# Modulation vectors by VectorE accumulation instead of TensorE products, in a two-layer diffusion trunk step

## The chip, the core and the metric

The kernel runs on one core of a Trainium2 chip, as one program. The metric is the device time of one execution in microseconds (us), as the median of three runs. Five engines work side by side: TensorE (PE in the profile; its weight loads are PEld), VectorE (DVE), ScalarE (ACT), GpSimd (POOL) and SyncE (SP), which here issues every DMA.

## The reference

Two segments of tokens, 128 context tokens and 512 latent tokens, pass the same two layers. Each segment has a conditioning vector; `adaln` turns it into six modulation vectors of 1024 per layer, which scale and shift what goes into the token mixer and the channel mixer and gate what comes out.

```
def adaln(cond, w, b):
    m = jax.nn.silu(cond) @ w + b                       # (1, 1024) @ (1024, 6 * 1024)
    return [m[:, None, i * D_MODEL:(i + 1) * D_MODEL] for i in range(N_MOD)]

def channel_mixer(hn, l, P):
    u = dwconv3(hn @ P['w_up'][l], P['conv_w'][l], P['conv_b'][l])
    val, gate = u[..., :D_FF], u[..., D_FF:]
    return (jax.nn.silu(gate) * val) @ P['w_down'][l]

def trunk_layer(x, mods, l, P, angs, ctx_k, ctx_v):
    sh1, sc1, g1, sh2, sc2, g2 = mods
    hn = rmsnorm(x, P['norm1_g'][l]) * (1 + sc1) + sh1
    mix, k, v = token_mixer(hn, l, P, angs, ctx_k, ctx_v)   # Fourier mixer + differential attention, gated
    x = x + g1 * mix
    hn = rmsnorm(x, P['norm2_g'][l]) * (1 + sc2) + sh2
    x = x + g2 * channel_mixer(hn, l, P)
    return x, k, v
```

## The kernel before

Activations lie transposed, channels on partitions and all 640 tokens along the free axis, in 53 general buffers ("slots", 128 x 640 in float32) that are handed out and taken back in turn. Every large product is computed in three float32r terms (high x high, high x low, low x high). A weight block of 1 MB is loaded into one of two raw tiles (`w_raw`), then split into `w_h` (ScalarE or GpSimd, line 311 or 313) and `w_l` (VectorE, line 317), four pieces of 128 x 512 each. `make_plan` lists the blocks in order; a block is loaded when the block two places ahead of it has been used (`pump_loads`).

The program goes, for each layer, through: a prologue or `layer_start` (norm, first key/query/value products), eight attention heads, the gate products with the Fourier mixer woven in, `merge`, `w_o`, then up and down products of the channel mixer in three rounds. TensorE's products are emitted in generators and loops that call `tick()` after each group of matmuls (one k-step of `proj`: six matmuls of 128 x 320); a tick emits one piece of the next weight's split and one of the waiting epilogue operations. In a head, softmax units of four steps alternate with stretches of the next projections as filler; how much filler stands between two steps is set by `cost(h)`. The order written there is a priority: the tile scheduler that builds the program places instructions in each engine's queue by it and by its own estimate of when each can start.

The modulation vectors of layer 0's first norm come from the prologue (`first_ada`). The other 20 blocks of 512 columns (8 of layer 0, 12 of layer 1) are cut in halves of 512 rows. A half is a 1 MB block in the same plan and the same two raw tiles as the weights. It is used unsplit: four matmuls in full float32, with 32 columns of `c_cond` as the stationary operand, each written to its own 32 partitions of a PSUM tile.

```
for j in range(4):
    self.mm(out=ps[32 * j:32 * j + 32, 0:512], lhsT=self.cs[:, 4 * r + j, :], rhs=w[j], tile_position=(0, 32 * j))
```

ScalarE copies the first half's sums out (line 407), VectorE adds the second's (line 411), and `columns` transposes the result back to channels on partitions (four transposes, lines 270 and 429). One half follows each key/query job, value job, Fourier-input job and gate job while there are any (`ada_next`), and in layer 0 also each weight block of the up jobs 1 to 4. So in each layer 12 halves (six blocks) stand in the heads and 4 in the gates, and 8 more in layer 0's up jobs.

The tables of rotary angles and of the Fourier matrices (`c_big`, 1280 KB) are loaded once and stay.

## Time and profile before

| | |
|---|---|
| median of three runs | 2242.63 us (2241.78 to 2243.69) |
| the profiled execution | 2242.44 us, of which 2240.7 us from its first to its last instruction |
| TensorE busy | 2185.7 us, 98% of the span |
| VectorE, ScalarE, GpSimd busy | 1225.3, 800.2 and 362.4 us |
| moved by DMA | 200.41 MB |

The 1.7 us outside the span are there in every execution, so a change of the span is a change of the time. Matmuls are pipelined: one that is shown with 0.31 us starts about 0.147 us after the one before it. What a group of matmuls costs is therefore read from start to start, and the busy time of a group in the listings is time in which at least one of them ran.

### The profile page before, as it was taken

The page shows a single profiled execution, that of the slowest core. Times are in us where ns is not written, and L with a number is a line of the kernel's source. Part 1 is how long each engine was busy: PE and PEld are TensorE (multiplying, and loading weights), DVE is VectorE, ACT ScalarE, POOL GpSimd, SP SyncE. Part 2 cuts the span into 40 slices and gives each one's busy share as a digit, 9 for nine tenths or more (in the row PEclk, how much of TensorE's full clock was granted, in tenths as well). Part 3 has the DMA queues.
Part 4 walks back from the last instruction along what each step waited for, and adds up shares of the span by engine and source line. Part 5 has one row for each costly group of instructions (what it writes and reads, how often), then busy time and mean ns, then how long its engine had stood idle before and what let it go on. Part 6 is the DMA issues. An engine that isn't in the chain of part 4 may idle for free.

```text
span 2240.7 us, 36749 instructions
## 1 busy us (share of the span) xinstructions
PE 2185.7 (98%) x15142; PEld 2102.7 (94%) x15142; DVE 1225.3 (55%) x2258; ACT 800.2 (36%) x1601; POOL 362.4 (16%) x560
## 2 busy tenths in 40 slices
PE   7999999999999999999999999999999999999998
PEld 5988989999999999999989888899999999999997
DVE  5776675225456544545476766742344765355454
ACT  4565564212134221313246666532211433122221
POOL 2122122001032000000051211210010410000001
PEclk9999999999999999999999999999999999999999
DMA  8222322222213332122212222222222122222221
GB/s 312 84 84 84 118 79 76 113 94 71 73 66 113 133 112 76 62 90 76 76 66 102 83 82 85 79 112 99 91 76 76 59 76 75 75 77 75 76 76 47
DMA packets 40631, 200.41 MB, mean 89 GB/s; under 512 B 4496, under 2 KB 12048, under 8 KB 19344
## 3 DMA queue, kind: packets, MB, share of 16 engines
q1 hardware_dynamic: 40464, 198.07, 25.1%
q8 instruction: 119, 1.95, 0.4%
q14 instruction: 48, 0.39, 0.1%
HBM read 193.33 MB, written 4.72 MB: 88 GB/s over the span
## 4 chain that ended last, share of the span: by engine, by line
PE 76%; issue 7%; DVE 5%; POOL 5%; ACT 5%; DMA 1%; SPq 0%; POOLq 0%; ACTq 0%; DVEq 0%
PE ps_d L267 43%; PE ps_t L267 16%; PE ps_s L267 16%; POOL slot L500 2%; POOL ors L703 1%; ACT slot L634 1%; PE ps_t L270 1%; DVE nm L632 1%; DMA slot<-in_w_first 1%; ACT slot L536 1%; ACT junk L701 1%; DVE slot L515 1%; POOL oms L702 1%; ACT slot L537 1%; DVE w_l L317 1%
## 5 line engine op out<-in xcount | busy, mean ns | idle before, releaser
L267 PE MATMUL ps_d<-slot,w_h 128*128 128x320 f32 x5056 | 983.5, 313 | 8.0 <-DVE slot L501 4.5
L267 PEld LDWEIGHTS ps_d<-slot,w_h 128*128 128x128 f32 x5056 | 795.5, 188 | 25.0 <-DVE slot L501 8.4
L267 PE MATMUL ps_d<-slot,w_l 128*128 128x320 f32 x2528 | 595.6, 310 | 2.6 <-DVE w_l L317 2.6
L317 DVE TENSOR_TENSOR w_l<-w_raw,w_h 128x512 fp32r<-128x512 f32 x520 | 360.9, 704 | 264.5 <-ACT w_h L311 155.1
L267 PEld LDWEIGHTS ps_d<-slot,w_l 128*128 128x128 f32 x2528 | 427.8, 188 | 2.9 <-DVE w_l L317 2.9
L311 ACT CAST w_h<-w_raw 128x512 fp32r<-128x512 f32 x308 | 188.3, 620 | 460.2 <-PE ps_d L267 236.0
L313 POOL TENSOR_SCALAR w_h<-w_raw 128x512 fp32r<-128x512 f32 x212 | 143.8, 680 | 1216.5 <-PE ps_d L267 626.9
L267 PE MATMUL ps_s<-slot,w_h 128*128 128x320 f32 x1376 | 265.2, 310 | 0.0
L267 PE MATMUL ps_t<-slot,w_h 128*128 128x320 f32 x1376 | 264.6, 309 | 0.0
L267 PEld LDWEIGHTS ps_t<-slot,w_h 128*128 128x128 f32 x1376 | 217.7, 188 | 1.7 <-ACT slot L945 0.8
L267 PEld LDWEIGHTS ps_s<-slot,w_h 128*128 128x128 f32 x1376 | 217.5, 188 | 1.7 <-ACT slot L945 1.7
L634 ACT ACTIVATE slot<-ps_s,nm 128x640 f32<-128x640 f32 (+1 forms) x160 | 113.7, 711 | 150.2 <-DVE nm L632 148.3
L267 PE MATMUL ps_s<-slot,w_l 128*128 128x320 f32 x688 | 164.9, 310 | 1.1 <-DVE w_l L317 1.1
L267 PE MATMUL ps_t<-slot,w_l 128*128 128x320 f32 x688 | 164.7, 309 | 0.0
L632 DVE TENSOR_REDUCE nm<-ps_s 128x1 f32<-128x640 f32 (+1 forms) x160 | 113.9, 712 | 56.7 <-PE ps_s L267 49.6
L267 PEld LDWEIGHTS ps_s<-slot,w_l 128*128 128x128 f32 x688 | 116.9, 188 | 1.6 <-DVE w_l L317 1.6
L940 DVE SCALAR_TENSOR_TENSOR slot<-ps_d,c_vecs,slot 128x511 f32<-128x511 f32 (+1 forms) x176 | 84.6, 541 | 60.7 <-ACT slot L945 60.7
L267 PEld LDWEIGHTS ps_t<-slot,w_l 128*128 128x128 f32 x688 | 117.0, 188 | 0.0
L267 PE MATMUL ps_s<-slot,slot 128*128 128x320 f32 x512 | 102.3, 322 | 10.2 <-ACT slot L634 10.1
L267 PEld LDWEIGHTS ps_s<-slot,slot 128*128 128x128 f32 x512 | 77.7, 189 | 30.6 <-ACT slot L634 19.3
L267 PE MATMUL ps_d<-w_h,slot 128*128 128x256 f32 x480 | 99.6, 288 | 0.6 <-DVE cols L429 0.6
L940 DVE SCALAR_TENSOR_TENSOR slot<-ps_s,c_vecs,slot 128x511 f32<-128x511 f32 x88 | 42.6, 542 | 87.3 <-ACT slot L945 87.3
(167 smaller groups left out, 2258.9 us busy)
## 6 DMA issues: line engine op xcount, KB each, us to landing
w_raw<-in_w_stream SPq DMA_DIRECT2D x164, 1024.0 KB, 4.9
slot<-in_w_first SPq DMA_DIRECT2D x32, 256.0 KB, 6.0
w_raw<-in_w_stream SPq DMA_DIRECT2D x8, 768.0 KB, 4.3
slot<-in_x_t SPq DMA_DIRECT2D x8, 320.0 KB, 6.2
out_y_t<-slot SPq DMA_DIRECT2D x8, 320.0 KB, 2.2
c_big<-in_t_big SPq DMA_DIRECT2D x1, 1280.0 KB, 9.4
slot<-in_k_t SPq DMA_DIRECT2D x16, 64.0 KB, 1.8
slot<-in_v_h SPq DMA_DIRECT2D x16, 64.0 KB, 1.9
```

The costliest lines, as they stand in the source:

```text
L267: return self.nc.tensor.matmul(**a)
L270: return self.nc.tensor.transpose(*a)
L311: nc.scalar.copy(out=h[:, a:b], in_=raw[:, a:b])
L313: nc.gpsimd.tensor_scalar(out=h[:, a:b], in0=raw[:, a:b], scalar1=1.0, scalar2=0.0, op0=ALU.mult, op1=ALU.add)
L317: nc.vector.tensor_sub(out=lo[:, a:b], in0=raw[:, a:b], in1=h[:, a:b].bitcast(F32))
L500: (eng or nc.gpsimd).tensor_scalar(out=tmp[:, a:b], in0=tmp[:, a:b], scalar1=A, scalar2=B, op0=ALU.mult, op1=ALU.add)
L515: lambda: nc.vector.stream_shuffle(tmp[:, 128:640], src, mask=SHUF),
L536: nc.scalar.copy(out=KD[m][a:b], in_=kr[a:b])
L537: nc.scalar.copy(out=KD[m][c:d], in_=kr[a:b])
L632: nc.vector.tensor_reduce(out=st["nm"][:, m:m + 1], in_=s_ap, axis=AX.X, op=ALU.max, negate=True)
L634: nc.scalar.activation(out=p[:, 0:n], in_=s_ap, func=AF.Exp, bias=st["nm"][:, m:m + 1], scale=1.0, accum_out=st["sum"][:, m:m + 1])
L940: nc.vector.scalar_tensor_tensor(out=y[:, o0:o1], in0=ps[:, 192 + i0:192 + i1], scalar=w, in1=y[:, o0:o1], op0=ALU.mult, op1=ALU.add)
```

## The change

The 40 halves leave the plan and TensorE. The weights of the modulation vectors become an input of their own (`w_ada`, 160 pieces of 128 x 512, 256 KB each), which passes a ring of four slots. For each piece and each of the two segments one step is emitted (`ada_step`): the piece times the segment's conditioning column, added to an accumulator of 128 x 512. The first of a block's eight pieces goes to ScalarE (a scaled copy), the other seven to VectorE (`scalar_tensor_tensor`). That makes 280 steps on VectorE and 40 on ScalarE. After two blocks, TensorE sums the four accumulators over partitions with four matmuls against 32 columns of ones, ScalarE copies the sums out, and four transposes bring both blocks back (`ada_rows`, `ada_columns`): ten times in all.

Steps are emitted in two kinds of stretch alone. In the gates of each layer 0.85 of one comes with each tick, for six blocks. In layer 0's channel mixer 0.25 of one comes with each tick, for eight blocks, and `ada_until` emits what is left before the last down round. The heads have no such work any more, and `cost(h)` loses its 1.2. The tables move to five slots, are given back after use and loaded again at the end of layer 0; there are 61 slots instead of 53.

```diff
-NSLOT = 53
+NSLOT = 61
...
+ADA_UPTO = ((6, 14), (20, 20))
+ADA_RATE = (.85, .25)
...
-    def ada(l, cb):
-        return [(("ada", l, cb, r), "ada", "w_ada", l, 512 * r, 4, [(512 * cb, 512)]) for r in range(2)]
...
+ADA = [(0, cb) for cb in range(4, 12)] + [(1, cb) for cb in (2, 3, 0, 1)] + [(1, cb) for cb in range(4, 12)]
...
+    def tables(self):
+
+        b = self.big = [self.alloc() for _ in range(5)]
+        for i, t in enumerate(b):
+            self.nc.sync.dma_start(out=t[:, 0:512], in_=self.I["t_big"][:, 512 * i:512 * i + 512])
...
         if self.q:
             self.q.popleft()()
+        self.beat += 1
+        self.ada_tick()
...
+    def ada_open(self, upto, rate):
+
+        self.ada_upto, self.ada_rate = 8 * upto, rate
+        if self.ada_n < self.ada_upto:
+            self.ada_ring = [self.alloc() for _ in range(4)]
+            self.ada_at = self.ada_n
+            for _ in range(4):
+                self.ada_load()
+
+    def ada_load(self):
+        n = self.ada_at
+        if n < self.ada_upto:
+            self.nc.sync.dma_start(out=self.ada_ring[n % 4][:, 0:512], in_=self.I["w_ada"][n // 8, n % 8])
+            self.ada_at += 1
+
+    def ada_step(self):
...
+        acc, x = self.ada_acc[2 * (b % 2) + c][:, 0:512], self.cs[:, k, c:c + 1]
+        if k == 0:
+            nc.scalar.activation(out=acc, in_=w, func=AF.Copy, scale=x)
+        else:
+            nc.vector.scalar_tensor_tensor(out=acc, in0=w, scalar=x, in1=acc, op0=ALU.mult, op1=ALU.add)
+        self.ada_c = 1 - c
+        if c:
+            self.ada_n += 1
+            self.ada_load()
+            if k == 7 and b % 2:
+                self.ada_sums.append((self.beat + 10, lambda b=b, acc=self.ada_acc: self.ada_rows(b - 1, acc)))
...
+    def ada_rows(self, b, acc):
+        nc = self.nc
+        ps, s = self.psq(), self.alloc()
         for j in range(4):
-            self.mm(out=ps[32 * j:32 * j + 32, 0:512], lhsT=self.cs[:, 4 * r + j, :], rhs=w[j], tile_position=(0, 32 * j))
...
+            self.mm(out=ps[32 * j:32 * j + 32, 0:512], lhsT=self.one, rhs=acc[j][:, 0:512], tile_position=(0, 32 * j))
+        self.give(*acc)
+        nc.scalar.copy(out=s[:, 0:512], in_=ps[:, 0:512])
+        self.ada_sums.append((self.beat + 3, lambda: self.ada_columns(b, ps, s)))
...
+    def ada_tick(self):
+        if self.ada_sums and self.beat >= self.ada_sums[0][0]:
+            self.ada_sums.popleft()[1]()
+        self.ada_credit += 0 if self.hold else self.ada_rate
+        if self.ada_credit >= 1:
+            self.ada_credit -= 1
+            self.ada_step()
...
-        yield from self.ada_next()
...
-        cost = lambda h: 1.2 + (13.1 + (7.9 if h % 2 == 0 else 5.3) if h < 6 else 13.1 if h == 6 else 26.2)
+        cost = lambda h: (13.1 + (7.9 if h % 2 == 0 else 5.3) if h < 6 else 13.1 if h == 6 else 26.2)
...
+        self.ada_open(ADA_UPTO[l][0], ADA_RATE[0])
         G = gates()
...
+        self.ada_until(ADA_UPTO[l][0])
         self.finish_a(l, 1)
...
+        self.ada_open(ADA_UPTO[l][1], ADA_RATE[1])
         self.ff = [None] * NFF
         self.up_first(l, hn2, hooks)
         for j in range(1, 5):
             self.up(l, j, hn2)
+        self.ada_until(8)
         self.down(l, 0)
...
         if l + 1 < DEPTH:
+            self.ada_until(ADA_UPTO[l][1])
+            self.tables()
```

The first place is TensorE's queue in the gates of layer 0, at the end of a gate job (`w_l` and `w_h` are its weights, `c_big` a Fourier table). Before:

```order
L267 MATMUL ps_d<-slot_519,w_h_93 128x320
L267 MATMUL ps_d<-slot_518,w_l_95 128x320 x2
L267 MATMUL ps_s<-w_raw_92,c_cond 32x512 x4
L267 MATMUL ps_t<-c_big,slot_4683 128x256 x4
L267 MATMUL ps_t<-c_big,xp 128x128 x2
L267 MATMUL ps_d<-slot_264,w_h_94 128x320
```

The same queue in the change, at the end of the third gate job, where the sums of the first two blocks stand (`c_one` are the ones, the slots the accumulators):

```order
L263 MATMUL ps_d<-slot_526,w_l_94 128x320 x2
L263 MATMUL ps_d<-slot_4098,c_one 32x512
L263 MATMUL ps_d<-slot_4099,c_one 32x512
L263 MATMUL ps_d<-slot_4311,c_one 32x512
L263 MATMUL ps_d<-slot_4312,c_one 32x512
L263 MATMUL ps_d<-slot_263,w_h_93 128x320
```

A half after each gate job is replaced by one such group for two whole blocks; there are three groups in the gates of a layer.

The second place is VectorE's queue in the last head, where softmax steps (maximum, reciprocal, factor, combination) take turns with splits. Before:

```order
L632 TENSOR_REDUCE nm<-ps_s 128x1
L643 RECIPROCAL r<-sum 128x2
L644 TENSOR_SCALAR c<-sum,r,c_lam_85 128x1
L646 SCALAR_TENSOR_TENSOR slot_3824<-slot_3825,c,slot_3824 128x640
L704 TENSOR_SCALAR on<-ps_t,r,ors 128x128
L317 TENSOR_TENSOR w_l_95<-w_raw_91,w_h_93 128x512
```

In the change, the last unit of the same head:

```order
L415 SCALAR_TENSOR_TENSOR slot_4099<-slot_4076,c_cond,slot_4099 128x512
L667 TENSOR_REDUCE nm<-ps_s 128x1
L415 SCALAR_TENSOR_TENSOR slot_4099<-slot_4077,c_cond,slot_4099 128x512
L313 TENSOR_TENSOR w_l_95<-w_raw_91,w_h_93 128x512
L678 RECIPROCAL r<-sum 128x2
L415 SCALAR_TENSOR_TENSOR slot_4099<-slot_4078,c_cond,slot_4099 128x512
L679 TENSOR_SCALAR c<-sum,r,c_lam_84 128x1
L415 SCALAR_TENSOR_TENSOR slot_4098<-slot_4075,c_cond,slot_4098 128x512
L681 SCALAR_TENSOR_TENSOR slot_3986<-slot_3987,c,slot_3986 128x640
L739 TENSOR_SCALAR on<-ps_t,r,ors 128x128
```

The scheduler has drawn the first steps of the gates forward, in between the links of the last softmax chain (seven of them up to this place).

The third place is SyncE's queue in the gates of layer 0. Before, it holds the alternating raw tiles alone, weights and halves in turn:

```order
L291 DMA w_raw_91<-in_w_stream 128x2048
L531 DMA out_state_kt<-kp 128x128
L291 DMA w_raw_92<-in_w_stream 128x2048
L291 DMA w_raw_91<-in_w_stream 128x2048 x2
L291 DMA w_raw_92<-in_w_stream 128x2048 x2
```

In the change:

```order
L399 DMA slot_4075<-in_w_ada 128x512
L399 DMA slot_4076<-in_w_ada 128x512
L399 DMA slot_4077<-in_w_ada 128x512
L399 DMA slot_4078<-in_w_ada 128x512
L287 DMA w_raw_91<-in_w_stream 128x2048
L399 DMA slot_4075<-in_w_ada 128x512
```

Eight to twelve loads of the ring, each of which waits for the steps that read the piece before, now stand between two loads of a weight block.

## Rows read from the trace of the kernel before

**Rows 1.** The page: the span, and each engine's busy time.
```profile
span 2240.7 us, 36749 instructions
PE 2185.7 (98%) x15142; PEld 2102.7 (94%) x15142; DVE 1225.3 (55%) x2258; ACT 800.2 (36%) x1601; POOL 362.4 (16%) x560
```

**Rows 2.** TensorE's waits over the whole span: waiting line, releaser, total, times, longest.
```profile
PE ps_s L267 <- ACT slot L634: 10.1, 17, 1.8
PE ps_t L270 <- DVE on L704: 7.4, 12, 0.8
...
PE ps_d L270 <- DVE slot L411: 2.9, 6, 0.6
```

**Rows 3.** TensorE's groups by line and shape: the halves, each of eight records.
```profile
L267 PE MATMUL ps_d<-w_raw,c_cond 128*32 128x512 f32 x256 | 36.2, 605 | 0.0
...
L267 PE MATMUL ps_s<-w_raw,c_cond 128*32 128x512 f32 x32 | 4.3, 605 | 0.0
L267 PE MATMUL ps_t<-w_raw,c_cond 128*32 128x512 f32 x32 | 4.3, 604 | 0.0
```

**Rows 4.** TensorE's timeline around one half in the gates (start, duration).
```profile
397.08 0.45 PE L267 MATMUL ps_d<-slot,w_l 128*128 128x320 f32 x2
...
398.50 0.86 PE L267 MATMUL ps_d<-slot,w_h 128*128 128x320 f32 x4
```

**Rows 5.** TensorE's timeline at one block's four transposes in the gates.
```profile
420.90 0.60 PE L270 MATMUL ps_d<-c_small,slot 128*128 128x128 f32 x4
421.26 0.83 PE L267 MATMUL ps_d<-slot,w_h 128*128 128x320 f32 x4
```

**Rows 6.** Windows of heads 2, 5, 6, layer 0: length; busy PE, PEld, DVE, ACT, POOL; clock; DMA.
```profile
146.94:183.56 36.62, 35.99 (x273) 34.25 (x272) 26.93 (x52) 22.27 (x55) 7.64 (x12) 1.00 0.33 114
...
261.06:301.40 40.34, 37.74 (x284) 34.65 (x282) 26.18 (x52) 24.57 (x63) 7.85 (x14) 1.00 0.19 66
301.40:333.57 32.17, 30.62 (x206) 26.79 (x206) 24.67 (x49) 20.20 (x54) 6.77 (x11) 1.00 0.29 98
```

**Rows 7.** VectorE's groups by line and shape (busy, mean ns; idle before, releasers).
```profile
L317 DVE TENSOR_TENSOR w_l<-w_raw,w_h 128x512 fp32r<-128x512 f32 x520 | 360.9, 704 | 264.5 <-ACT w_h L311 155.1 <-POOL w_h L313 107.3 <-PE ps_d L267 1.5
...
L646 DVE SCALAR_TENSOR_TENSOR slot<-slot,c,slot 128x640 f32<-128x640 f32 x64 | 57.9, 905 | 1.9
...
L567 DVE SCALAR_TENSOR_TENSOR slot<-slot,slot 64x512 fp32r<-64x512 f32 x32 | 21.9, 686 | 3.9 <-ACT slot L562 3.1
```

**Rows 8.** Windows of layer 0's gates and of its first up jobs, columns as in rows 6.
```profile
384.00:512.00 128.00, 128.00 (x870) 122.79 (x870) 32.06 (x64) 32.98 (x55) 9.41 (x15) 1.00 0.25 91
690.00:830.00 140.00, 140.00 (x960) 131.72 (x959) 80.34 (x147) 43.03 (x60) 12.76 (x18) 1.00 0.36 131
```

**Rows 9.** The chain that ended last: one Fourier group's products, one gate job.
```profile
404.05 1.44 PE ps_s L267 x12
...
409.12 2.17 PE ps_t L267 x12
...
440.91 14.08 PE ps_d L267 x96
```

**Rows 10.** Timelines of GpSimd and of VectorE in the seventh head.
```profile
326.95 1.28 POOL L517 TENSOR_TENSOR slot<-slot,c_big 128x512 f32<-128x512 f32 x1
...
327.35 1.56 DVE L646 SCALAR_TENSOR_TENSOR slot<-slot,c,slot 128x640 f32<-128x640 f32 x1
```

**Rows 11.** The page's DMA issues: count, size, median us from issue to landing.
```profile
w_raw<-in_w_stream SPq DMA_DIRECT2D x164, 1024.0 KB, 4.9
slot<-in_w_first SPq DMA_DIRECT2D x32, 256.0 KB, 6.0
...
slot<-in_k_t SPq DMA_DIRECT2D x16, 64.0 KB, 1.8
```

**Rows 12.** Windows of 4 us in the fourth head, columns as in rows 6.
```profile
212.00:216.00 4.00, 2.57 (x19) 2.19 (x17) 3.16 (x6) 2.71 (x6) 0.74 (x2) 1.00 0.02 4
216.00:220.00 4.00, 3.61 (x14) 3.62 (x15) 2.20 (x4) 2.59 (x7) 0.00 (x0) 0.57 0.06 16
```

More of the change, by code (lines that the diff above doesn't have):

```diff
@@ L98, in make_plan @@
         v(l, 0)
-        for cb in range(4, 12):
-            adaq.extend(ada(l, cb))
         for h in range(8):
@@ L194, in __init__ @@
         self.small = mk("c_small", [128, 128])
-        self.big = mk("c_big", [128, 2560])
         self.ident = self.small
-        b = self.big
-        self.cos, self.sin = b[:, 0:512], b[:, 512:1024]
-        self.csj = b[:, 1024:1280]
-        self.c128, self.s128 = b[:, 1280:1408], b[:, 1408:1536]
-        self.ttab = [b[:, 1536 + 256 * i:1792 + 256 * i] for i in range(4)]
-        self.one = mk("c_one", [128, 1])
+        self.one = mk("c_one", [128, 32])
         self.mh = mk("c_mh", [128, 6])
@@ L225, in __init__ @@
         self.cur = 0
-        self.wseq = [i for i in range(self.n) if self.plan[i][3] == "w"]
+        self.wseq = list(range(self.n))
         self.wpos = {i: j for j, i in enumerate(self.wseq)}
@@ L388, in vtile @@
                 yield 0.66
-    def ada_next(self):
-        if self.plan[self.cur][3] != "ada":
-            return
-        _, l, cb, r = self.plan[self.cur][0]
-        i, raw = self.begin("ada", l, cb, r)
-        yield from self.ada_half(l, cb, r, [raw[:, j, :] for j in range(4)], lambda: self.finish_raw(i))
-    def ada_half(self, l, cb, r, w, after):
+    def ada_open(self, upto, rate):
[5 more added lines that the diff above has]
+                self.ada_load()
@@ new lines, in ada_load @@
+    def ada_load(self):
[4 more added lines that the diff above has]
+    def ada_step(self):
+        n, c = self.ada_n, self.ada_c
+        if n >= self.ada_upto:
+            return False
+        nc, w = self.nc, self.ada_ring[n % 4][:, 0:512]
+        b, k = divmod(n, 8)
+        if k == 0 and c == 0:
+            self.ada_acc += [self.alloc(), self.alloc()]
+        acc, x = self.ada_acc[2 * (b % 2) + c][:, 0:512], self.cs[:, k, c:c + 1]
[9 more added lines that the diff above has]
+                self.ada_sums.append((self.beat + 10, lambda b=b, acc=self.ada_acc: self.ada_rows(b - 1, acc)))
+                self.ada_acc = []
+            if self.ada_n == self.ada_upto:
+                self.give(*self.ada_ring)
+        return True
@@ L400, in ada_half @@
+    def ada_rows(self, b, acc):
         nc = self.nc
-        ps = self.psa()
+        ps, s = self.psq(), self.alloc()
         for j in range(4):
-            self.mm(out=ps[32 * j:32 * j + 32, 0:512], lhsT=self.cs[:, 4 * r + j, :], rhs=w[j], tile_position=(0, 32 * j))
-        after()
-        if r == 0:
-            self.half = self.alloc()
-            nc.scalar.copy(out=self.half[:, 0:512], in_=ps[:, 0:512])
-            yield 0.92
-            return
-        s = self.half
-        nc.vector.tensor_add(out=s[:, 0:512], in0=s[:, 0:512], in1=ps[:, 0:512])
@@ new lines, in ada_rows, with ada_columns @@
+        self.give(*acc)
+        nc.scalar.copy(out=s[:, 0:512], in_=ps[:, 0:512])
+        self.ada_sums.append((self.beat + 3, lambda: self.ada_columns(b, ps, s)))
+    def ada_columns(self, b, ps, s):
+        for j in range(4):
+            self.tr(ps[:, 512 + 128 * j:640 + 128 * j], s[:, 128 * j:128 * j + 128], self.ident)
+        self.give(s)
+        part = ps[:, 512:1024].rearrange("p (b g r) -> p b g r", b=4, g=4)
+        for i in range(2):
+            l, cb = ADA[b + i]
+            bcol = self.vec[4][:, 48 * l + 4 * cb:48 * l + 4 * cb + 4]
+            self.nc.vector.tensor_tensor(out=self.mods[l][:, 4 * cb:4 * cb + 4, :], in0=part[:, :, 2 * i:2 * i + 2, 0],
+                                         in1=bcol.rearrange("p (j o) -> p j o", o=1).to_broadcast([128, 4, 2]), op=ALU.add)
@@ L422, in columns, with ada_until @@
+    def ada_until(self, n):
+        while self.ada_n < 8 * n and self.ada_step():
+            pass
+        while self.ada_sums:
+            self.ada_sums.popleft()[1]()
+    def ada_tick(self):
+        if self.ada_sums and self.beat >= self.ada_sums[0][0]:
+            self.ada_sums.popleft()[1]()
+        self.ada_credit += 0 if self.hold else self.ada_rate
+        if self.ada_credit >= 1:
+            self.ada_credit -= 1
+            self.ada_step()
     def columns(self, ps, c0, s):
@@ L465, in rstd_cols @@
         for i, t in enumerate(starts):
-            self.mm(out=ps[:, c0 + i:c0 + i + 1], lhsT=self.acc[:, t:t + 128], rhs=self.one)
+            self.mm(out=ps[:, c0 + i:c0 + i + 1], lhsT=self.acc[:, t:t + 128], rhs=self.one[:, 0:1])
         ms, rs = self.tiny("ms", 6), self.tiny("rs", 6)
@@ L620, in v_job @@
         self.v_epi(l, p, ps, 0, 4, 1)
-        yield from self.ada_next()
     def unit(self, l, h, qt):
@@ L966, in up @@
                 self.up_epi(l, g, m, ps, yv)
-            self.run(self.ada_next())
     def up_epi(self, l, g, m, ps, yv):
@@ L1308, in layer @@
             self.give(*pair)
+        self.give(*self.big[0:2])
         prev[1]()
@@ L1333, in layer @@
             some(1.6)
+        self.give(*self.big[2:5])
         some(1e9)
@@ L1354, in layer @@
         if l + 1 < DEPTH:
+            self.ada_until(ADA_UPTO[l][1])
+            self.tables()
             hn = [(self.alloc(F32R), self.alloc(F32R)) for _ in range(8)]
```

37 lines of the change are left out of this document (10 added, 27 removed).

## The prediction

> **What bounds the kernel.** I read the page first: TensorE is busy for 98% of the span, VectorE for 55% [rows 1]. A busy TensorE need not be a full one, so I then read its cadence and its waits. In the gates it starts a 128 x 320 matmul every 0.147 us without a gap: 96 of them take 14.08 us [rows 9]. Over the whole span its listed waits on attention's softmax chain come to some 10.1 and 7.4 us, and it waits 2.9 us for the modulation blocks' own addition on VectorE [rows 2]. Nothing else is large. So a microsecond of TensorE work that goes is a microsecond of time, except where a chain of other engines takes over; the heads are the only place with such waits in number, so I read their windows one by one [rows 6].
>
> **What is removed from TensorE.** The halves have 320 records, eight each: 40 halves. Their busy time is 36.2 + 4.3 + 4.3 = 44.8 us [rows 3], 1.12 us each. The timeline agrees: the pair of ordinary matmuls before a half starts at 397.08 and would be followed 0.29 us later, and the next ordinary matmul starts at 398.50, which leaves 1.13 us for the half [rows 4]. Each of the 20 blocks also has four transposes, 0.36 us from start to start [rows 5]: 7.2 us. Together 52.0 us.
>
> **What TensorE gets instead.** Ten groups of four products with ones, of the same shape, precision and column placement as a half, so 1.12 us each, and ten times four transposes at 0.36 us: 14.8 us. The three groups in a layer's gates stand at ticks that lie after their accumulators' last steps by VectorE's load below, so I add no wait for the accumulators. Net removal: 52.0 - 14.8 = **37.2 us**, and up to 2.9 us of waits on the blocks' own additions [rows 2]; I count 2 us of these, since a chain that stands behind such a wait may take some of it over.
>
> **What the heads give back.** Of the removal, 24 halves and 12 times four transposes stood in the heads of both layers: 24 x 1.12 + 12 x 0.36 = 31.2 us, and they were filler between softmax steps. Is the filler needed? Head 2 has 22.2 units of filler by its cost line and TensorE is idle 0.63 us of its 36.62; head 6 has 14.3 and is idle 1.55 us of 32.17 [rows 6]. So 7.9 units less cost 0.92 us of idleness, 0.12 us per unit. At that slope 31.2 us less give back 3.6 us. The bounds are nothing and twice that: head 5, with 19.6 units, is idle for 2.6 us [rows 6], so filler is not all that matters.
>
> **What VectorE gets.** 280 steps of 128 x 512 with both tensors in SBUF. No such step is in the trace. The nearest rows are the subtraction of 128 x 512 (mean 0.704 us), the scalar-tensor-tensor of 64 x 512 (0.686 us) and that of 128 x 640 (0.905 us, or 0.72 us by size) [rows 7]. I take 0.69 us, bounds 0.67 and 0.91 us. 280 x 0.69 = 193 us on an engine with 1015 us free. Per stretch: in a layer's gates there are 6 x 14 = 84 steps, 58 us on top of 32.1 us busy in 128 us [rows 8], that is 70%. In a gate job of 14.08 us [rows 9] the ticks bring 0.85 x 16 x 7/8 = 11.9 steps, 8.2 us, beside four splits, 2.8 us. What is left of the 32.1 us after eight jobs' splits, 9.7 us, is the Fourier mixer's for the most part: 2.4 us for each of four groups, and each group also brings TensorE 1.44 + 2.17 = 3.6 us more [rows 9]. It fits: VectorE may run a microsecond or two late. What is late next is the split of the next weight block, and that has a whole job of 14 us for 2.8 us of work, so TensorE does not see it. In the up jobs an up tile of 7.04 us gets 1.75 steps, 1.2 us, and VectorE goes from 57% [rows 8] to 74%; four PSUM tiles lie between TensorE and the epilogues. I cost both at nothing. Without that cover, at a mean step of 0.91 us, the gates would still be at 32.1 + 76 = 108 of 128 us.
>
> **What the hoisted steps cost.** In the last head seven steps stand between links of the softmax chain. Each can hold a link by at most 0.69 us: 9.7 us in both layers at worst, nothing at best. VectorE is busy for about 70% of a head (24.67 to 26.93 of 32 to 40 us [rows 6]), and the scheduler put them where it thought the engine free; I take 1 us per layer, 2 us.
>
> **What the ring and SyncE cost.** SyncE's queue now holds eight to twelve ring loads between two weight loads, and each waits for the step that last read its slot, so a late VectorE also holds the weight loads behind it. When a piece is used up, three pieces, six steps, 7.1 ticks or 6.2 us lie before its slot is needed again. A 64 KB load lands in 1.8 us and a 1024 KB one in 4.9 us; the 256 KB loads of the prologue, issued in a row behind others, in 6.0 us [rows 11]. A ring load alone is thus nearer to 2.5 us (an estimate by size between the first two). Behind a weight load it reaches about 6 us, once per job. I cost it at nothing. The page "DMA: Bandwidth & Descriptors" of the Trainium skill (section Bandwidth) speaks against this part of the change: it wants loads of 1 MiB or more, for three quarters of the peak rate. No sum here changes by it, because the gates ask for less than the rate at which the 1024 KB loads land; if ring loads took the time of a whole 1 MB each, the case is that of a late VectorE below.
>
> **Waits of other kinds.** The groups in the gates take a turn in the PSUM rotation in the middle of a job, so the next tile may wait for the tile just finished to be copied out. Six groups at about the mean wait of rows 2 (0.6 us) would be 3.6 us at most; I take 1 us. The tables' second load (five pieces in place of one of 1280 KB) lies a whole down round ahead of its use, and its slots come from the long end of the free list: nothing.
>
> **The sum**, against the profiled execution's own 2242.44 us (0.2 us under the median): 2242.4 - 37.2 - 2 + 3.6 + 2 + 1 = 2209.8, so **2210 us**. With every gain and no cost it is 2242.4 - 37.2 - 2.9 = 2202.3; with every cost at its upper bound and no waits saved, 2242.4 - 37.2 + 7.2 + 9.7 + 3.6 = 2225.7.
>
> **Rivals.**
>
> *The heads keep half of it.* Were the softmax chain the bound of most units, filler taken out would come back as waiting. For it: 17 waits for the exponentials and 12 for the normalised output [rows 2]. Against it: the small difference between heads 2 and 6. There is an amplifier: in the fourth head, after 1.43 us of idleness within 4 us, the granted clock of the next 4 us is 0.57, the lower of TensorE's two levels (1.2 instead of 2.4 GHz) for most of them [rows 12]; one such fall costs about 0.43 x 4 = 1.7 us, and there could be more. Half of 31.2 us lost: 2242.4 - 37.2 + 15.6 + 3.4 for two falls = 2224 us.
>
> *VectorE is late in the gates.* The step reads two tensors from SBUF, and such instructions can take twice their time while GpSimd works: a combination of 128 x 640 took 1.56 us beside a GpSimd product that ran from 326.95 to 328.23 [rows 10], against a mean of 0.905. "GPSIMD Engine Reference" of the Trainium skill (section Specifications) says as much: GpSimd shares its SBUF interface with VectorE, which meets contention when it has two SBUF inputs; the trace agrees with it at this place. GpSimd is busy 9.41 us of the gates' 128 us [rows 8], so only some 7% of the steps should meet it. Spread over the eight jobs, VectorE has 32.1 / 8 + 11.9 d = 4.0 + 11.9 d per job against 14.1 + 4 x 3.6 / 8 = 15.9 us of TensorE work, d being the mean step; VectorE becomes the bound of the gates at d = 1.0 us. At d = 1.07 it would be 0.8 us per job over 16 jobs, 13 us: 2210 + 13 = 2223 us.
>
> *Slower than before.* The same mechanism from d = 1.17 us on: (4.0 + 13.9 - 15.9) x 16 = 32 us, about what is won. If every step met GpSimd, at twice 0.69 us, it would be (4.0 + 16.4 - 15.9) x 16 = 72 us: 2282 us. The gates' 7% of GpSimd speaks clearly against it.
>
> **Chances.** The forecast 0.76; the heads keep half 0.11; VectorE late but still a gain 0.08; slower or the border to it 0.05. A difference of 0.2%, 4.5 us, is about what a measurement of this kernel can tell from none. Faster than that: 0.94 (the first three, less a hundredth); within it 0.02; slower 0.04. The range is 2201 to 2225 us: about the bounds of the sum, which take in most of the second case and part of the third.
>
> **What would show it.** TensorE's listing has no product from `w_raw`, 80 records with `c_one` of 128 x 512 and about 11 us. VectorE has 280 scalar-tensor-tensors from the ring at 0.67 to 0.75 us mean and is busy for about 1400 us. Gate jobs still take 14.08 us with TensorE at 100% of the gates' window; the heads' windows are shorter by some 1.1 us per half removed, with idleness up by a few tenths each. The forecast is wrong if TensorE waits for ring steps or for `w_l` in the gates, if waits on lines of the softmax chain exceed 25 us in all, or if windows of the heads show more granted clock below 1.00.

## The result: 2212 us, and where the time came from

The changed kernel takes 2212.41 us (median of four runs, 2211.09 to 2214.10) against 2243.16 us for the kernel before in the same measurement; the ratio is 0.9863, with an interval of 0.9846 to 0.9881. The forecast was 2210 us, range 2201 to 2225. The profiled executions took 2214.1 us (the longest of the four; 2.1 us of it lie outside the span) and 2242.44 us.

The page of the changed kernel, to be held against [rows 1]:

```profile
span 2212.0 us, 36833 instructions
PE 2157.3 (98%) x14862; PEld 2099.6 (95%) x14862; DVE 1388.6 (63%) x2498; ACT 816.1 (37%) x1631; POOL 387.6 (18%) x560
```

TensorE's busy time fell by 28.4 us and the span by 28.7. VectorE got 163 us more, as the forecast had it (about 1400).

The moved work itself, in the changed kernel: TensorE's groups of products with ones (answering to [rows 3]), VectorE's group of ring steps (to [rows 7]) and the page's DMA issues (to [rows 11]).

```profile
L263 PE MATMUL ps_d<-slot,c_one 128*32 128x512 f32 x40 | 5.3, 604 | 0.0
L263 PE MATMUL ps_s<-slot,c_one 128*32 128x512 f32 x24 | 5.3, 605 | 0.0
L263 PE MATMUL ps_t<-slot,c_one 128*32 128x512 f32 x16 | 2.1, 604 | 0.0
...
L415 DVE SCALAR_TENSOR_TENSOR slot<-slot,c_cond,slot 128x512 f32<-128x512 f32 x280 | 204.1, 772 | 11.6 <-DMA slot<-in_w_ada 10.3 <-ACT slot L413 0.8
...
w_raw<-in_w_stream SPq DMA_DIRECT2D x124, 1024.0 KB, 4.9
slot<-in_w_ada SPq DMA_DIRECT2D x160, 256.0 KB, 2.9
```

A step takes 0.772 us in the mean (forecast 0.69, bounds 0.67 and 0.91; the sign that it named was 0.67 to 0.75), and 0.745 in the median. The trace shows what lifts the mean: 58 of the 280 steps run while a GpSimd instruction is under way and take 0.878 us in the mean, 1.128 at most; the other 222 take 0.744 us, 0.754 at most. In the gates it is 38 of 168 steps, 23%, where the prediction expected 7%. Ring loads land in 2.9 us; VectorE waited 10.3 us for them in all, and no line of TensorE's waits names a ring load or a ring step. The products take 12.7 us, not 11.2. The row with `ps_s` shows why: 24 records cost as much as the 40 with `ps_d`. In the third group of each layer's gates one product was drawn ahead alone; layer 0's timeline of TensorE has it here, between the end of ordinary products and their return:

```profile
458.55 0.60 PE L266 MATMUL ps_d<-c_small,slot 128*128 128x128 f32 x4
459.08 1.04 PE L263 MATMUL ps_s<-slot,c_one 128*32 128x512 f32 x2
460.06 0.71 PE L263 MATMUL ps_d<-slot,w_h 128*128 128x320 f32 x3
```

From 459.08 to 460.06 that one product holds TensorE for 0.98 us. A whole group of four, each on its own 32 columns, lies between 418.45 and 419.44, 0.99 us. The Trainium skill, "TensorEngine Tiling (Array Packing)", section Tiling Modes, says that different tiles of the array can run matmuls in parallel; the trace agrees, and the other side of it is that a lone one saves nothing.

TensorE's waits over the whole span, against [rows 2]:

```profile
PE ps_t L266 <- DVE on L739: 11.2, 22, 1.3
PE ps_d L263 <- DVE slot L875: 5.4, 4, 2.7
PE ps_t L266 <- DVE slot L681: 4.1, 10, 0.5
PE ps_s L263 <- POOL rs L506: 3.9, 1, 3.9
```

The waits on the blocks' own additions (2.9 us) are gone, and those for the exponentials have fallen from 10.1 to 1.3 us. Two lines are new in size: `L875`, the update of the residual from a PSUM tile, and one single wait of 3.9 us for `rs` of a norm.

**By stage.** I cut the executions at marks that all of them share: the first product with `c_pq` (the first head's start) and each `rs` of GpSimd (the reciprocal root of a norm's mean square `ms`; twice in the norm inside `w_o`, twice in the norm at the end of a layer). All lengths in us, each from the trace of one execution; the three columns on the right are experiments that follow.

| stretch | before | changed | both repairs | no vectors | steps twice |
|---|---|---|---|---|---|
| prologue | 73.61 | 75.28 | 72.65 | 75.64 | 75.33 |
| layer 0, heads to first rs | 570.42 | 552.96 | 552.96 | 545.78 | 560.83 |
| norm in `w_o`, rs to rs | 22.17 | 26.14 | 22.24 | 22.12 | 26.11 |
| layer 0, channel mixer | 459.90 | 456.58 | 455.63 | 448.48 | 455.76 |
| norm at its end, rs to rs | 22.80 | 26.48 | 21.94 | 21.84 | 26.35 |
| layer 1, heads to first rs | 571.73 | 554.97 | 554.96 | 548.01 | 563.32 |
| all the rest of layer 1 | 520.07 | 519.59 | 519.92 | 519.43 | 520.20 |

Where two kernels hold the same work, the attention parts repeat to some 0.2 us from execution to execution; the mixer, the norm behind it and the last row vary by 0.5 to 1.2 us, and the prologue by up to 5. The change won 17.46 and 16.76 us in the two attention parts, where the forecast's sum comes to 14.06 each (16 halves and 8 times four transposes less, 20.8; three groups more, 4.44; and half of each of its four other terms, 2.3). Against that, 3.97 and 3.68 us were lost in two norms of layer 0 that no term of the sum speaks of.

**The first loss.** In the norm in layer 0's `w_o`, the second `rs` needs a short link on VectorE, `ms`. Before the change, `ms` starts 0.7 us after its sums are ready (at 665.3), and TensorE's products with `rs` follow without a listed wait:

```profile
665.97 0.15 DVE L468 TENSOR_SCALAR ms<-ps_t 128x3 f32<-128x3 f32 x1
...
667.11 0.93 PE L267 MATMUL ps_t<-c_small,rs 128*128 128x128 f32 x6
```

In the changed kernel, the timeline of the same place (VectorE, GpSimd and TensorE), and the windows of 4 us around it:

```profile
650.16 4.06 DVE L415 SCALAR_TENSOR_TENSOR slot<-slot,c_cond,slot 128x512 f32<-128x512 f32 x6
...
654.14 0.16 DVE L505 TENSOR_SCALAR ms<-ps_s 128x3 f32<-128x3 f32 x1
...
654.38 1.29 POOL L506 TENSOR_TENSOR rs<-ms,c_mh 128x3 f32<-128x3 f32 x1 [8.54 <-DVE ms L505]
...
655.72 1.65 PE L263 MATMUL ps_s<-c_small,rs 128*128 128x128 f32 x6 [3.86 <-POOL rs L506]
```
```profile
652.00:656.00 4.00, 0.28 (x1) 0.29 (x2) 3.61 (x7) 0.00 (x0) 1.29 (x1) 0.77 0.93 364
656.00:660.00 4.00, 4.00 (x17) 4.00 (x18) 2.45 (x5) 2.04 (x4) 0.85 (x1) 0.50 0.39 128
660.00:664.00 4.00, 4.00 (x26) 4.00 (x25) 2.99 (x6) 2.60 (x6) 4.00 (x5) 0.88 0.00 0
```

Six ring steps of the mixer, drawn forward by the scheduler, stand in VectorE's queue ahead of the 0.16 us that the norm's chain needs. The sums for it were ready at about 650; `ms` starts at 654.14, `rs` after it, and TensorE waits 3.86 us. Then the granted clock is 0.50, the lower of its two levels, and a window of 4 us holds 17 records, not about 30.

**The second loss.** At the end of layer 0, TensorE's first products for layer 1 need PSUM tiles that VectorE has to empty first. Before the change one of them waits for that:

```profile
1138.76 0.56 PE L267 MATMUL ps_d<-slot,w_h 128*128 128x320 f32 x2 [1.17 <-DVE slot L842]
```

In the changed kernel two do, for longer; below them VectorE's updates that release them, and the windows of 4 us there:

```profile
1123.17 0.53 PE L263 MATMUL ps_d<-slot,w_h 128*128 128x320 f32 x2 [1.23 <-DVE slot L875]
...
1126.59 0.90 PE L263 MATMUL ps_d<-slot,w_h 128*128 128x320 f32 x2 [2.74 <-DVE slot L875]
```
```profile
1122.49 0.54 DVE L875 SCALAR_TENSOR_TENSOR slot<-ps_d,c_mods,slot 128x320 f32<-128x320 f32 x1
...
1125.99 0.55 DVE L875 SCALAR_TENSOR_TENSOR slot<-ps_d,c_mods,slot 128x320 f32<-128x320 f32 x1
```
```profile
1124.00:1128.00 4.00, 1.41 (x5) 1.41 (x6) 3.38 (x6) 0.98 (x2) 4.00 (x6) 0.65 0.44 115
1128.00:1132.00 4.00, 4.00 (x17) 4.00 (x16) 3.47 (x9) 0.98 (x2) 0.52 (x2) 0.50 0.41 166
```

No ring step is near. But each group of sums takes a turn in the rotation of PSUM tiles (`psq`: d, d, s, t), as a half did in its place outside the heads. Before, layer 0 had 4 such turns in its gates and 8 in its up jobs, 12, a multiple of four; now it has 3 and 4, and its last down round begins one place earlier in the rotation. Its last four tiles are then t, d, d, s, and not d, d, s, t. Layer 1 starts the rotation anew (`layer_start` sets `psi` to 0) with d, d: now just the tiles finished last but two and last but one. So it waits for their updates, which stand in VectorE's queue among the splits of normalised chunks.

**The heads** (windows of heads 2, 5 and 6, against [rows 6]):

```profile
145.69:179.15 33.46, 32.91 (x252) 32.35 (x251) 25.23 (x49) 21.80 (x56) 6.07 (x10) 1.00 0.20 70
...
250.83:288.67 37.84, 36.79 (x273) 35.22 (x271) 24.95 (x49) 23.22 (x61) 8.52 (x14) 1.00 0.10 36
288.67:321.33 32.66, 31.11 (x212) 28.33 (x210) 23.94 (x47) 21.80 (x55) 6.07 (x10) 1.00 0.20 67
```

Idle time did not rise: 0.55, 1.05 and 1.55 us, after 0.63, 2.60 and 1.55. The filler that left was not missed, or something paid for it. The fall of the clock in the fourth head [rows 12] has no counterpart: in the changed kernel's heads every window of 4 us has a granted clock of 1.00.

### The profile page after: what moved, and what is told of

Same layout as the page of the kernel before. It is cut to its first block, busy times and chain, and to the rows that moved or that the text cites. A ratio compares the mean times of both kernels' runs of the same rounds, so it can differ in the third digit from the quotient of the medians.

```text
span 2212.0 us, 36833 instructions
## 1 busy us (share of the span) xinstructions
PE 2157.3 (98%) x14862; PEld 2099.6 (95%) x14862; DVE 1388.6 (63%) x2498; ACT 816.1 (37%) x1631; POOL 387.6 (18%) x560
## 4 chain that ended last, share of the span: by engine, by line
PE 76%; issue 7%; DVE 6%; POOL 5%; ACT 5%; DMA 1%; SPq 0%; ACTq 0%; POOLq 0%; DVEq 0%
PE ps_d L263 43%; PE ps_s L263 16%; PE ps_t L263 15%; POOL slot L537 2%; POOL ors L738 2%; PE ps_t L266 2%; DVE nm L667 1%; ACT slot L669 1%; DMA slot<-in_w_first 1%; ACT junk L736 1%; DVE on L739 1%; POOL oms L737 1%; ACT slot L573 1%; DVE slot L415 1%; DVE slot L681 0%
## 5 line engine op out<-in xcount | busy, mean ns | idle before, releaser
L263 PE MATMUL ps_d<-slot,w_h 128*128 128x320 f32 x5088 | 997.0, 313 | 9.5 <-DVE slot L875 5.4
L263 PEld LDWEIGHTS ps_d<-slot,w_h 128*128 128x128 f32 x5088 | 804.1, 189 | 21.9 <-DVE slot L538 5.4
L263 PE MATMUL ps_d<-slot,w_l 128*128 128x320 f32 x2544 | 604.3, 311 | 2.6 <-DVE w_l L313 2.6
L309 POOL TENSOR_SCALAR w_h<-w_raw 128x512 fp32r<-128x512 f32 x212 | 156.0, 737 | 1173.3 <-PE ps_d L263 598.6
L263 PE MATMUL ps_t<-slot,w_h 128*128 128x320 f32 x1344 | 259.7, 310 | 0.5 <-DVE slot L538 0.5
L263 PEld LDWEIGHTS ps_t<-slot,w_h 128*128 128x128 f32 x1344 | 212.9, 188 | 3.0 <-DVE slot L538 1.0
L415 DVE SCALAR_TENSOR_TENSOR slot<-slot,c_cond,slot 128x512 f32<-128x512 f32 x280 | 204.1, 772 | 11.6 <-DMA slot<-in_w_ada 10.3
L263 PE MATMUL ps_s<-slot,slot 128*128 128x320 f32 (+2 forms) x592 | 114.5, 318 | 2.7 <-ACT slot L669 1.3
L263 PEld LDWEIGHTS ps_s<-slot,slot 128*128 128x128 f32 x592 | 87.3, 188 | 12.6 <-ACT slot L669 10.6
```

Source lines behind the costliest of these rows:

```text
L263: return self.nc.tensor.matmul(**a)
L309: nc.gpsimd.tensor_scalar(out=h[:, a:b], in0=raw[:, a:b], scalar1=1.0, scalar2=0.0, op0=ALU.mult, op1=ALU.add)
L415: nc.vector.scalar_tensor_tensor(out=acc, in0=w, scalar=x, in1=acc, op0=ALU.mult, op1=ALU.add)
```

## The experiments

The theory: TensorE's lighter load is the gain, and two side effects of the new work's order cost some 9 us. Rivals: the clock, VectorE itself or the loads cost it.

### Steps kept behind the norm

```diff
-        nc.vector.tensor_scalar(out=ms[:, 0:n], ...)
+        self.behind = nc.vector.tensor_scalar(out=ms[:, 0:n], ...).ins
...
-            nc.vector.scalar_tensor_tensor(out=acc, in0=w, scalar=x, in1=acc, op0=ALU.mult, op1=ALU.add)
+            with self.tc.issue_after(self.behind): nc.vector.scalar_tensor_tensor(out=acc, in0=w, ...)
```

> The changed kernel with one edit: every ring step is issued behind the mean-square instruction (TENSOR_SCALAR ms) of the norm that was traced last, so in layer 0's norm inside w_o the six ring steps no longer stand ahead of it on VectorE. Theory: those 4.06 us of steps are what made TensorE wait 3.86 us for rs and then run a stretch at the lower clock level. Then the time from the first to the second rs of that norm falls from 26.14 us to about 22.2 (before: 22.17), the granted clock around 652 to 664 us is 1.0, and the time falls by about 5 us, to 2207. The six steps now stand between ms and the normalising products, so up to 2 us may come back as a wait on those. Rival: the other rotation of the PSUM tiles (ps_s in place of ps_t) is what makes this norm late; then the 26.14 us and 2212 stay. Second rival: the drop of the clock comes by itself, whatever PE did; then the wait goes, the drop stays, and the time falls by 3.5 us at most.

Measured: 2207.83 us, ratio to before 0.9844 (0.9831 to 0.9858). From rs to rs it is 22.27 us, the granted clock is 1.00 in each window of 4 us from 650 to 666, and the wait for `rs` is gone. In a second version the steps stand behind the norm's last product with the rows tile (`self.behind` set there too):

> As the run before, but the ring steps are issued behind the last product of the normalised chunk with the rows tile, so no step stands anywhere inside the norm. Theory: as before 22.2 us from rs to rs and no wait of TensorE in the first up tiles; 2207 us or 1 to 2 us under the run before if its steps delayed the normalised chunk. Rival (the steps behind ms were free): the same time as the run before. The steps now start 5 to 9 us later in the mixer; were they needed early there, TensorE would wait for the first group's sums, which stands far behind.

Measured: 2205.71 us, 0.9834 (0.9821 to 0.9848). This norm:

```profile
648.62 0.14 DVE L505 TENSOR_SCALAR ms<-ps_s 128x3 f32<-128x3 f32 x1
...
650.14 0.83 PE L263 MATMUL ps_s<-c_small,rs 128*128 128x128 f32 x6
```
```profile
650.00:654.00 4.00, 4.00 (x31) 4.00 (x30) 2.01 (x5) 2.43 (x5) 1.25 (x2) 1.00 0.56 229
654.00:658.00 4.00, 4.00 (x30) 4.00 (x29) 2.77 (x7) 1.36 (x3) 3.88 (x4) 1.00 0.00 0
```

Norm and mixer together take 477.80 us, after 482.72 in the changed kernel: 4.9 us for the wait and the clock. The rotation was untouched, so the rival of the PSUM tiles falls for this norm; and the drop of the clock went with the wait. Between the two versions the trace has 0.6 us (478.44 and 477.80); in the profiled executions the rest of their difference lies mostly in the prologue (75.93 and 73.79), and the intervals overlap. That the steps behind `ms` cost 1 to 2 us is not borne out.

### The rotation set back

```diff
-            self.tables()
+            self.tables(); self.psi = 0
             hn = [(self.alloc(F32R), self.alloc(F32R)) for _ in range(8)]
```

> The changed kernel with one edit: the counter of the PSUM rotation is set to 0 ahead of layer 0's last down round, so its last four tiles are d, d, s, t as before the change, not t, d, d, s. Theory: the tiles that layer 1's first projection takes (d, d) are then free 4 to 8 us earlier; the waits of 1.23 and 2.74 us for L875 shrink to one of about 1.2, the clock stays at 1.0 around 1124 to 1132, the time from rs to rs falls from 26.48 to about 22.8, and the total by 3.7 us, to about 2208.7. Rival: VectorE itself is late there, behind scaled chunks that share GpSimd's port; then the waits move to the tiles' new names and the time stays at 2212. Second rival: the second load of the tables competes there; the time stays too.

Measured: 2209.06 us, 0.9849 (0.9836 to 0.9862), 3.35 us under the changed kernel. From rs to rs it is 21.84 us. TensorE's wait at the place, and the window after it:

```profile
1122.47 0.56 PE L263 MATMUL ps_d<-slot,w_h 128*128 128x320 f32 x2 [0.63 <-DVE slot L875]
```
```profile
1124.00:1128.00 4.00, 4.00 (x28) 3.82 (x27) 3.37 (x6) 0.98 (x2) 3.97 (x6) 1.00 0.60 182
```

VectorE's updates stand as late as before (1121.88, 1125.40, 1127.51); only the tiles that layer 1 takes first are others. The tables' second load stayed in its place, so it is not the cause. In the six other versions that keep the changed kernel's rotation this norm takes 25.3 to 26.3 us, with the same two waits; in the version without any group of sums, below, it takes 21.84, as here.

### Both together

> Steps behind the norm and the rotation reset together. Theory: the two losses lie in different stretches and add: 2212.4 - 5 - 3.7 = about 2203.5 us, if the prologue keeps its drop of the clock (28 to 40 us), and 1.7 us less if that drop was one execution's alone. Rival: one of the two gains only moves a wait to the next stretch; then 2207 to 2209.

Measured: 2202.76 us (2201.38 to 2204.19), ratio 0.9821 (0.9807 to 0.9834): 9.65 us under the changed kernel and 40 under the one before. The gains add, and in the table they stand in the two norms and, with 0.95 us, in the mixer behind the first of them. Between the prologue and the last 13 us, the changed kernel has windows of 4 us with a granted clock below 1.00 at these two norms alone; with both repairs there is none.

### Without the moved work

```diff
     def ada_open(self, upto, rate):
-        self.ada_upto, self.ada_rate = 8 * upto, rate
+        return
```

> The changed kernel without the modulation work that it moved: no ring loads, no steps, no sums (the vectors of the later blocks are set to zero; the first norm's stay). It shows what the moved work still costs in all. Theory: TensorE's ten groups (12.7 us of products and 3.6 of transposes), the wait and the clock of layer 0's norm (about 4.9) and the rotation at the end of layer 0 (about 3.7 to 4.6) are all of it, VectorE's 204 us and the 160 loads are hidden: 2212.4 - 16.3 - 4.9 - 4 = about 2187. Rival: the steps or the loads also cost something spread out, in the last heads or in the gates, by splits and epilogues that come later; then it is lower, 2182 or less.

Measured: 2182.81 us (2182.49 to 2183.11), ratio 0.9736 (0.9721 to 0.9750). Both theories missed by 0.8 to 4 us; the rival is the nearer. With the two losses repaired (2202.8) the moved work costs 20 us by the medians and 21.3 by the stages, where TensorE's ten groups at 1.48 us each come to 14.8. By the table, three groups in a layer's gates cost 7.18 and 6.95 us, 2.4 each; four in the mixer 7.15, 1.8 each. Of a layer's 7.1 us, 4.4 are the groups at the forecast's price, 0.8 a longer wait in the last head (waits on `L739` from there to the first rs 2.7 us, without the steps 1.9), and up to 0.98 the lone product; the last 0.9 us or so I can't assign.

### The sums kept together

```diff
-        for j in range(4):
-            self.mm(out=ps[32 * j:32 * j + 32, 0:512], lhsT=self.one, ...)
+        with self.tc.issue_after(self.last):
+            for j in range(4): self.mm(out=ps[32 * j:32 * j + 32, 0:512], lhsT=self.one, ...)
```

> The kernel with both repairs (steps behind the norm, rotation reset), and each group of four products with ones issued behind the product traced before it, so that no single product of the third group of the gates is drawn forward alone. Theory: four products side by side take 1.0 us and a single one as long; a lone one in each layer's gates costs 0.98 us, so the products' busy time falls from 12.7 to 10.6 us and the time by 2 us: 2200.8. Rival: the drawn-forward product filled a gap that TensorE had there anyway; then the time stays at 2202.8.

Measured: 2202.25 us (2199.56 to 2203.12), 0.9819 (0.9806 to 0.9832). The products fell to 10.6 us (the `ps_s` row to 3.2), and the two attention parts to 552.43 and 554.66 us, 0.5 and 0.3 less: a third to a half of the 0.98. On the time it can't be told from none. By its median it is the fastest kernel here that does the whole computation.

### What pays for the heads' missing filler

Two things left the heads beside the filler: the halves' copies on ScalarE, and the 1.2 in `cost(h)`. One run puts back ten copies per layer (128 x 512, results not used), one the 1.2, one both.

```diff
-        self.later(*self.q_epi(ps, l, h))
+        self.later(*self.q_epi(ps, l, h)); self.copy_only()
...
-        self.v_epi(l, p, ps, 0, 4, 1)
+        self.v_epi(l, p, ps, 0, 4, 1); self.copy_only()
```
```diff
-        cost = lambda h: (13.1 + ...
+        cost = lambda h: 1.2 + (13.1 + ...
```

> The changed kernel plus ten ScalarE copies of 128 x 512 per layer, one after each key/query and value job of the heads, where before the change the halves and their copies stood; the copies' results are not used. The question is why the heads gave nothing back when 31.2 us of filler left TensorE (their idle time in layer 0 fell from 10.5 to 6.7 us). Theory: the halves' own work on ScalarE had held up the exponentials (waits 10.1 us before, 1.3 us after), so what the missing filler cost was paid by what their copies no longer delay. Then with the copies back the waits of TensorE for the exponentials rise to 6 us or more, the seven heads of layer 0 take 2 to 4 us longer than the 246.05 us of the changed kernel, and the time is 2216 to 2219. Rival: the halves held TensorE's own order (a PSUM d tile each), not ScalarE; then the copies hide, the waits stay near 1.3 us, and the time stays at 2212.

> The changed kernel with the 1.2 put back into cost(h), so that the filler is spread over the five units of a head as if a half still stood in it: each stretch is filled a little earlier and the last one has less. Theory: how the filler is spread matters little, heads 246 us within 1 us, time 2212 within 1.5. Rival: the lower waits of the heads after the change come from the new spread, not from the halves' absence; then the waits for the exponentials return towards 10 us, and the time rises by 3 to 6 us.

> The changed kernel with both the ten ScalarE copies per layer in the heads and the 1.2 in cost(h). Apart, the copies lengthened the seven heads by 1.85 and 2.42 us (layer 0 and 1), the 1.2 by 1.63 and 1.93. Theory: two separate causes, which add: the heads take about 249.5 and 252.6 us, against 246.05 and 248.21 in the changed kernel, and the time is about 2220 (2212.4 + 7.8). With both put back the heads would then give back some 3 us per layer of the filler that was removed, more than the forecast had. Rival: both act on the same waits of the softmax chain; then the two together are worth little more than one, 248 and 250.7 us, 2216.

Measured: copies 2214.63 us, the 1.2 2216.55 us, both 2215.95 us (ratios 0.9879, 0.9884, 0.9881). The seven heads take 247.90, 247.68 and 247.86 us in layer 0 (changed kernel 246.05), and 250.63, 250.14 and 250.20 in layer 1 (248.21). Each alone costs about 2 us per layer, both together no more: the gain needed both to go, and the forecast priced neither. In the trace they look different. With the copies the listed waits for the exponentials in layer 0's seven heads are 1.2 us (changed kernel 0.7) and TensorE's idle time there rises only from 6.7 to 7.2 us, while eight more of its matmuls fall into these heads; with the 1.2 the waits are 2.3 us and the idle time 8.5. Both waits are far from the 5.0 before, and from the 6 that the copies' theory wanted. So the numbers come out as the last run's rival had them, but that both act on the same waits is not shown.

Lowering `cost(h)` by another 1.2 (with both repairs, and then with the sums kept together as well) shows how sharp that setting is:

> The kernel with both repairs, and cost(h) lowered by another 1.2, so that the filler of a head starts later and more of it is left for its end. The 1.2 that the change took out was worth 1.6 to 1.9 us per layer. Theory: it goes on in this direction, but with less: the heads take 245 to 246 us in layer 0 and the time is 2201 to 2202. Rival: the optimum is passed, since the last units then keep filler after their softmax chain is done: 248 us and 2206.

> The two runs before in one kernel. Theory: they lie in different stretches and add, 2199 to 2200.5; rival: the lowered cost loses, then 2204.

Measured: 2225.94 us (0.9927, 0.9914 to 0.9939) and 2224.20 us (0.9918, 0.9905 to 0.9932). The heads take 256.4 us in layer 0 and 259 in layer 1. The first of the two, TensorE's waits:

```profile
PE ps_s L263 <- ACT slot L669: 17.9, 30, 1.4
PE ps_t L266 <- DVE on L739: 6.9, 14, 0.9
```

TensorE waits for the exponentials again, 17.9 us in all after 1.3 in the changed kernel. The theory that it would go on in this direction was wrong by 24 us and its rival by 20; why 1.2 less has so large an effect, no run shows.

### Every ring step twice

```diff
-            nc.vector.scalar_tensor_tensor(out=acc, in0=w, scalar=x, in1=acc, op0=ALU.mult, op1=ALU.add)
+            for _ in range(2): nc.vector.scalar_tensor_tensor(out=acc, in0=w, scalar=x, in1=acc, ...)
```

> The changed kernel with each of VectorE's 280 steps issued twice (the sums come out wrong by it), so that a step costs about 1.47 us. It tests where VectorE becomes the bound. By the formula of the prediction a gate job then has 4.0 + 11.9 x 1.47 = 21.5 us of VectorE against 15.9 us of TensorE: 5.6 us per job over 16 jobs, 90 us, or 2300. Rival: VectorE's backlog can spill over the end of the gates into the sums, and the steps drawn forward into the last head start the gates early; then each layer's gates last as long as its 84 steps and the rest of VectorE's work in them, 84 x 1.47 + 32 + 4 = 160 us against 128, 60 us for both layers, and the time is about 2275. Third: the scheduler spreads them so that less than half of this shows, 2230 to 2250.

Measured: 2228.38 us, 0.9940 (0.9925 to 0.9955). The two attention parts are 7.9 and 8.4 us longer, 16 in all, not 90 and not 60; the third theory came nearest. A doubled step takes 1.54 us (twice a mean of 0.772). Windows of layer 0's last head and gates, first of the changed kernel, then, somewhat later, with the steps doubled:

```profile
381.00:411.00 30.00, 30.00 (x204) 29.48 (x203) 24.25 (x49) 9.91 (x18) 3.97 (x8) 1.00 0.57 185
411.00:441.00 30.00, 30.00 (x206) 28.70 (x205) 28.37 (x47) 9.17 (x16) 3.90 (x4) 1.00 0.65 210
441.00:471.00 30.00, 30.00 (x201) 27.96 (x200) 11.86 (x19) 7.87 (x12) 2.52 (x4) 1.00 0.24 83
```
```profile
441.44:471.44 30.00, 28.85 (x195) 27.25 (x194) 30.00 (x46) 7.10 (x11) 4.71 (x5) 1.00 0.44 143
471.44:497.44 26.00, 26.00 (x175) 24.90 (x173) 26.00 (x39) 9.82 (x16) 5.72 (x3) 1.00 0.39 133
497.44:521.44 24.00, 20.78 (x127) 17.99 (x126) 22.80 (x35) 6.27 (x10) 5.98 (x4) 1.00 0.26 88
```

The third column of busy times is VectorE's. In the changed kernel it is nearly full up to 441 us and then at 40%: the scheduler has drawn the steps forward, and they run from 351.7 us, in the last head, to 445.3. Doubled, they run to 500 us and fill VectorE until then, and TensorE is idle for 3.2 us in the window where the third group's sums fall due, and for 1.2 us in the first of the three. Some 8 us over 84 steps is 0.1 us each, so the gates have room for about 1.4 us per step (an estimate from this one run).

## Why the forecast came out right, and what in it was wrong

- **The removal and the groups.** 52.0 us of halves and transposes off TensorE hold: per attention part 16 halves and 8 times four transposes are 20.8 us by the forecast's prices, and the kernel without the vectors is 24.64 and 23.72 us shorter there than before. The rest, 3.8 and 2.9 us, is about the 1.2 in `cost(h)` (worth 1.9 and 2.2 us from the heads to the first rs) and the waits on the blocks' own additions (1.4 us per layer). The groups were under-sized: with all that hangs on them 2.4 us in the gates and 1.8 in the mixer, not 1.48. That is 6.5 us in all, of which the forecast had 3 under hoisted steps and turns in the rotation.
- **"What the heads give back" failed as a term.** It put 3.6 us back, 1.8 per layer, by a slope between two heads. With the 1.2 left in, the attention parts are 15.58 and 14.53 us shorter than before. Adding what the moved work costs there (7.18 and 6.95) gives 22.8 and 21.5 us, where the removal and the waits on additions come to 22.2. So the heads gave back -0.6 and 0.7 us (an estimate by difference): the term was too large. And what left the heads beside the filler was costed at nothing without being named: the 1.2 in `cost(h)`, a line of the diff, and the halves' copies. With both gone the attention parts came out 3 us per layer better than the sum.
- **"What the hoisted steps cost" looked at one place of two.** In the last head it took 1 us per layer, measured 0.8 and 0.6. The same scheduler drew mixer steps into the norm of `w_o`, ahead of a chain that TensorE waits for with nothing behind it: 4.9 us.
- **"Waits of other kinds" priced a group's turn in the rotation, not what it leaves behind.** The turns in the gates cost no listed wait, but the phase that they leave cost 3.7 us at the end of layer 0 (4.6 against the rotation set back).
- **VectorE, the ring and SyncE** cost TensorE little beyond that, as forecast, for reasons partly other than given. VectorE's load is not 70% through the gates but 81 to 95% from 381 to 441 us, then 40% and less to 491. GpSimd met more steps than expected, but at 1.5 times the undisturbed time at most, not twice. The rival's formula (bound from 1.0 us per step) gives 103 us at 1.54, and the run with doubled steps shows 16: it charged 11.9 steps to each of eight jobs, 95 where there are 84, and left out that they start in the last head.

In the profiled execution the attention parts came out 6 us better than the sum, layer 0's norms and mixer 9 us worse, and the prologue 1.7 us longer. So that the number is right within 2.4 us is partly luck: errors of 6 and 9 us nearly cancelled. The mechanism, a TensorE that is the bound and gets less work, and its largest term held.

## What to carry to other kernels

Work that a scheduler may place freely has no price of its own: look in the built order for every place where it stands ahead of a short link of a chain, and fasten it behind that link. When an edit adds or drops turns of a rotating set of buffers, count the turns modulo its length and look at who takes the next buffers after it, however far away. And price every constant that the change touches: 1.2 in a filler's cost was worth 4 us in one direction and 23 in the other.

## What the runs showed of the hardware

TensorE's granted clock fell after waits: after 3.86 us of waiting a whole window of 4 us ran at 0.50, and after 1.23 and 2.74 us the same. Before the change, the fall in the fourth head [rows 12] followed a single wait of 1.81 us:

```profile
216.39 1.34 PE L267 MATMUL ps_s<-slot,slot 128*128 128x320 f32 x4 [1.81 <-ACT slot L634]
```

In the changed kernel's heads, where the listed waits are 0.7 us at the longest and 1.3 in the last one, the clock stays at 1.00, and so it does in the heads of the version with the lowered cost, with waits of up to 1.4 us. With the waits at the two norms taken away or down to 0.8 us, it stayed at 1.00 there. In the norm of `w_o` wait and clock together cost 4.9 us, which by subtraction is about 1 us more than the wait.

A ring step (two inputs in SBUF) was slow only beside GpSimd: in every version that has ring steps, those clear of any GpSimd instruction take 0.757 us at most, and all longer ones, up to 1.173 us, overlap one.

The prologue's length varies by itself. Its program is the same in all changed versions (but for the memsets in the one without the vectors and one early copy in the two with copies), and the first head began between 70.76 and 75.93 us after the start. Windows of the changed kernel, then of the version with the sums together and the lowered cost:

```profile
32.00:36.00 4.00, 2.49 (x9) 2.09 (x9) 4.00 (x9) 0.00 (x0) 0.00 (x0) 0.50 1.05 387
36.00:40.00 4.00, 4.00 (x19) 4.00 (x19) 2.77 (x8) 1.20 (x3) 0.60 (x2) 0.53 1.05 387
```
```profile
32.00:36.00 4.00, 2.95 (x19) 2.74 (x19) 4.00 (x9) 0.00 (x0) 0.00 (x0) 1.00 1.05 385
36.00:40.00 4.00, 4.00 (x33) 2.43 (x34) 1.96 (x7) 2.64 (x6) 1.85 (x3) 1.00 1.05 388
```

TensorE waits for the first weights there, DMA is at its full share, and whether the clock falls in between differs from execution to execution, and the first head starts up to 5 us apart. What decides it stays open. Differences of 1 to 2 us between two kernels of this study should therefore be read by stage, not from the total.
